# Ordering each strand's loads behind its own last product, and loading the RWKV bonus at the end of a pair's norm

## The chip, the cores and the metric

The kernel runs on one NeuronCore of one Trainium2 chip. The metric is the device time of one execution in microseconds (us). The kernel before takes 959.26 us, the median of 3 runs between 958.56 and 960.78 us. Its engines are TensorE (PE, with the load of its stationary operand shown apart as PEld), VectorE (DVE), ScalarE (ACT), GpSimd (POOL) and SyncE (SP), which here does little but issue transfers.

## What is computed

A hybrid decoder block on one sequence of 512 tokens and a width of 1024, in fp32. One input projection feeds two head groups: eight heads of sparse attention (compressed, selected and window branches with gates) and eight heads of RWKV-7 time mixing. Their outputs go through one output projection `w_out`; then come cross-attention into 256 memory tokens, a SwiGLU feed-forward part and a final norm.

```
h   = rms_norm(x, g1)
nsa = attention(q, k_cmp, v_cmp, k_sel, v_sel, k_win, v_win, gates)   # 8 heads
rw  = rwkv7(h)                 # state chain over time, group norm, + bonus, * gate
x   = x + concat(nsa, rw) @ w_out
x   = x + cross_attention(rms_norm(x, gx), rms_norm(mem, gm) @ w_kv_x) @ w_o_x
x   = x + swiglu(rms_norm(x, gf));  out = rms_norm(x, g_final)
```

The bonus of RWKV is a term of each head pair that is computed early, stored to DRAM (tile `bdr`), and added at the end of that pair's norm.

## The kernel before, in words

All of x stays on the chip. Weights come in blocks of 512 KB. A block has a raw tile `w` (two buffers), and is split into two halves: ScalarE casts it to `wh` (line 339) and VectorE subtracts to get `wl` (line 340); `wh` and `wl` have two buffers each. A product with a weight is three matmuls (line 207): high by high, high by low, low by high. A raw buffer is free for another load when the `wl` of its block is done, and a `wh` or `wl` buffer is free when TensorE has made the last product with it.

The order of work is written by a planner in the program (class `Threads`). The work is a set of generators, called strands: the bulk strand (all weight products in a fixed list), one for each attention unit, one for the RWKV inverse and chain, one for the memory tokens, and more. At each `yield` the planner takes the strand of highest priority that is ready, on a clock that it adds up from estimated product times. `pin` puts each TensorE instruction behind the one before it of the same strand (`mine[th.cur]`) and remembers it as the last of any strand (`last[0]`). These are edges of order only, for the list scheduler that writes the five instruction streams; they are no semaphores on the chip. `now` gives such an edge to a DMA. It is used by `wload` (every weight load, line 373), by the stores and loads of the bonus (lines 650 and 848), by the gate weight `gup` (line 844) and by a few smaller loads.

All these DMAs are issued by SP in one stream. Around 200 us the bulk strand ends the input projection (`pj`); the RWKV inverse stores its result to DRAM (`ydr`, `xdr`, lines 729 and 730) and loads it back in another layout (`AM`, `X`, lines 742 and 738). Small products `lt` and `y` follow, and then the chain of eight steps (`ch`, `zy`). From 300 us the bulk strand makes K of the memory tokens (`kx`, 8 blocks) and then V (`vx`, 4 blocks shown below), beside the attention units (`ps` scores, `pt` transposes, `pv` values; `S` the probabilities on ScalarE and VectorE) and the four RWKV norms (line 842 on). Then comes `w_out` (`acc`), whose first accumulators use the PSUM banks of `vx`. The x rows for the residual (`xr`, 4 times 512 KB, line 1317) are loaded by SP between the second and the third block of `w_out`.

Of the kernel before, what the change touches and what calls it, by code (L numbers as in the profile page):

```python
# [14 lines left out]
T = 512  # L15
# [112 lines left out]
def _body(ctx, tc, I, out, dbg=None, upto=99, mark=lambda s: None):  # L128
    nc = tc.nc
# [13 lines left out]
    def mk(tag, bufs, pool=None):  # L143
        def f(shape=(128, 512), dt=F32, n=tag):
            return (pool or pp).tile(list(shape), dt, tag=tag, bufs=bufs, name=nm(n))
        return f
# [9 lines left out]
    tU = mk("U", NU)  # L156
# [9 lines left out]
    th = Threads(mark, lambda n: tc.high_priority(n) if n else nullcontext(), Q=NQ - 7, T=NT, U=NU, K=KU, S=2, A=2)  # L166
# [4 lines left out]
    def after(ins, first):  # L171
        tc.add_manual_dep(ins.ins, first.ins.name,
                          mybir.DependencyInfo(mybir.DependencyClass.NoSync, mybir.DependencyReason.DATA), reason="order")
        return ins

    last, mine = [None], {}
# [8 lines left out]

    def now(ins):

        return after(ins, last[0]) if last[0] is not None else ins

    def free(ap):  # L190
        n = 1
# [4 lines left out]
    def mm(o, l, r, start, stop):  # L196
        m, n = free(l), free(r)
        if l.dtype == F32R:
            c = (0.055 if m <= 64 else 0.107) if n <= 128 else n * 0.000422
        elif m <= 32:  # L200
            c = 0.04
        elif m <= 64:
            c = max(0.08, n * 0.0009 + 0.02)
        else:
            c = max(0.214, n * 0.00168)
        th.cols.append((th.clock, n * l.shape[0] / 128 * (1 if l.dtype == F32R else F4)))
        return pin(PE.matmul(o, lhsT=l, rhs=r, start=start, stop=stop, skip_group_check=True), c)  # L207
# [130 lines left out]
    def split(H, L, src, eng=None):  # L338
        seq(A, A.copy(H, src))  # L339
        i = (eng or V).tensor_sub(L, src, v32(H))  # L340
        if not eng:
            seq(V, i)
# [22 lines left out]
    def qpair(n):  # L365
        t = tQ([128, 2, 512], F32R, n=n)
        return t[:, 0, :], t[:, 1, :]

    def wload(parts, kt, cols, dst=None):

        w = tW([128, kt, cols], n="w")
        for sl, c0, s in parts:
            now(nc.sync.dma_start(w[sl, :, c0:c0 + s.shape[2]], s))

        def halves(eng=None):
            h, l = dst or (tH([128, kt, cols], F32R, n="wh"), tL([128, kt, cols], F32R, n="wl"))
            with th.ahead(PR.get("split", 0)):
                split(h, l, w, eng)
            return h, l
        return halves  # L380
# [170 lines left out]
    def bsum(x, n, al):  # L551

        H, L = al(dt=F32R, n="bh"), al(dt=F32R, n="bl")
        split(H, L, x)
        yield 2.5
        p = pS(n=n)
        mm(p, bones_r, H, True, False)
        mm(p, bones_r, L, False, True)
        yield p
# [11 lines left out]
    bdr = dp.tile([4, 128, 512], F32, name="bdr")  # L571

    def rwkv_pair(j):
# [74 lines left out]
        v_ = rkv[j, 2]  # L648
        V.tensor_mul(t, p, v_)
        now(nc.sync.dma_start(bdr[j], t))  # L650
        th.free(T=1)
        yield dict(Q=2)

        am2 = []
        for e in range(2):
            am = tQ([128, 8, 128], n="AM")
            sl = slice(e * 64, e * 64 + 64)
            for hf in range(2):
                p = pB(n="sc")
                for c in range(4):  # L660
                    cc = hf * 4 + c
                    for o in range(2):
                        mm(p[o * 64:o * 64 + 64, c * 128:(c + 1) * 128], bk[sl, cc, o ^ e, :], ar[sl, cc, :], True, True)
                V.tensor_tensor(am[:, hf * 4:hf * 4 + 4, :], p.rearrange("p (c t) -> p c t", c=4),
                                mask2.rearrange("p (o t) -> p o t", o=1).broadcast_to([128, 4, 128]), op=ALU.mult)
                yield 0
            am2.append(am)
            for hh in range(2):
                now(nc.sync.dma_start(ndv[hh, e, j], am[e * 64 + hh * 32:e * 64 + hh * 32 + 32, :, hh * 32:hh * 32 + 32]))
# [109 lines left out]
    def chain():  # L779
        yield "vt"  # L780

        def own(q):

            for c in (2 * q, 2 * q + 1):
                for j, e, o in HEADS:
                    r = slice(64 - o, 128 - o)
                    mm(pE[o:o + 64, c % 2, j, :], AM[j][e][r, c, 0:64], VT[c // 4][r, c % 4, j, :], True, True)
            z = tU([128, 2, 4, 64], n="zv")
            A.copy(z, pE)
            return z  # L790

        yield "vg"
        yield dict(A=1)
        pE = pA([128, 2, 4, 64], n="zy")
        zv = own(0)
        yield CH_LAG
        p = pC([128, 2, 4, 64], n="ch")
        S = None
        for c in range(8):

            uv = tU([128, 2, 4, 64], n="uv")
            G.tensor_copy(uv[64:128, 0], VT[c // 4][64:128, c % 4])
            G.tensor_copy(uv[0:64, 1], VT[c // 4][0:64, c % 4])
            if c > 0:
                for j, e, o in HEADS:
                    mm(p[o:o + 64, 0, j, :], AR[j][o:o + 64, c, 0:64], S[o:o + 64, j, :], True, True)
                Z = t1([128, 4, 64], n="Z")
                V.tensor_add(Z, p[:, 0], zv[:, c % 2])
            else:
                Z = zv[:, 0]  # L810
            if c % 2 == 1 and c < 7:
                zv = own(c // 2 + 1)
            if c > 0:
                yield CH_LAG
            for j, e, o in HEADS:
                mm(p[o:o + 64, 1, j, :], AM[j][e][o:o + 64, c, 0:64], Z[o:o + 64, j, :], True, True)
            V.tensor_copy(uv[0:64, 0], p[0:64, 1])
            A.copy(uv[64:128, 1], p[64:128, 1])
            if c > 0:
                for j, e, o in HEADS:  # L820
                    mm(pE[o:o + 64, c % 2, j, :], S[o:o + 64, j, :], AR[j][o:o + 64, c, 64:128], j == 0, False)
            yield CH_LAG

            Sn = None
            if c < 7:
                for j, e, o in HEADS:
                    mm(p[o:o + 64, 0, j, :], BKt[j][:, c, e, :], uv[:, e, j, :], True, True)
                Sn = t1([128, 4, 64], n="S")
                if c == 0:
                    V.tensor_copy(Sn, p[:, 0])  # L830
                else:
                    G.tensor_tensor(Sn, S, WC[:, :, c:c + 1].broadcast_to([128, 4, 64]), op=ALU.mult)
                    V.tensor_add(Sn, p[:, 0], Sn)
            for j, e, o in HEADS:
                mm(pE[o:o + 64, c % 2, j, :], uv[:, e, j, :], AM[j][e][:, c, 64:128], c == 0, True)
            A.copy(VT[c // 4][:, c % 4], pE[:, c % 2])
            S = Sn
            yield CH_LAG
        th.done("chain", 1.0)
        th.free(Q=16, U=4, A=1)  # L840

        yield dict(Q=1)
        gup = tQ([128, 512], n="gup")
        now(nc.sync.dma_start(gup, I["rwkv_g_up"][0]))
        for j in range(4):
            yield dict(U=3, T=2)
            bon, sq, rs = tU(n="bon"), tU(n="ysq"), tU(n="rs")
            now(nc.sync.dma_start(bon, bdr[j]))
            h2 = [slice(0, 256), slice(256, 512)]
            c4 = lambda x: x.rearrange("p (c t) -> p c t", c=4)  # L850
            for h in range(2):
                A.activation(c4(sq[:, h2[h]]), VT[h][:, :, j, :], AF.Square)
            bs = bsum(sq, "var", tT)
            yield next(bs) + 1.0
            yield dict(s=1)
            p = next(bs)
            th.free(T=2)
            A.activation(rs, p, AF.Ln, bias=kst[:, 1:2], scale=1.0 / 64)
            A.activation(rs, rs, AF.Exp, scale=-0.5)
            for h in range(2):  # L860
                V.tensor_mul(c4(rs[:, h2[h]]), c4(rs[:, h2[h]]), VT[h][:, :, j, :])
            V.tensor_scalar(rs, rs, col("rwkv_lnx_w", j), col("rwkv_lnx_b", j), op0=ALU.mult, op1=ALU.add)
            G.tensor_tensor(rs, rs, bon, op=ALU.add)
            yield 6.0
            yield dict(s=1)
            p = pS(n="g")
            mm(p, gup[:, j * 128:(j + 1) * 128], sgd, True, True)
            V.tensor_mul(rs, p, rs)
            yield dict(Q=1)
            oT[4 + j] = qpair("oT")  # L870
            split(*oT[4 + j], rs)
            th.free(U=3)
            th.done(f"o{4 + j}", 4.0)
        th.free(Q=3)
# [765 lines left out]
```

## Time and profile before

| | us |
|---|---|
| median of the runs | 959.26 |
| the profiled execution's own time | 957.83 |
| its span, first to last instruction | 955.5 |
| TensorE busy | 910.5 (95%) |
| VectorE busy | 508.4 (53%) |
| ScalarE busy | 401.2 (42%) |
| GpSimd busy | 81.7 (9%) |

The span is 2.33 us shorter than the time of the same execution; these lie before the first and behind the last instruction. A row of a timeline is one instruction, or several alike in a row (x2), with its start, its duration, the engine, the source line and the tiles (out<-in); the bracket at its end is the idle time of the engine before it and what ended it. A row of a window gives for each engine how long it was busy in that stretch. TensorE's clock is shown as a share of full speed.

### The profile page before, as it was taken

What the parts mean: (1) busy time and instruction counts of PE and PEld (TensorE: products, weight loads), DVE (VectorE), ACT (ScalarE), POOL (GpSimd) and SP (SyncE); (2) the same over time, 40 slices, a digit from 0 to 9 for tenths busy, and PEclk for the clock granted to TensorE, in tenths of its full rate; (3) what the DMA queues carried; (4) which work ended last, traced back from release to release, by engine and by line L of the source; (5) the groups of instructions that cost most, each with busy time, mean ns of one, the idle gap of its engine ahead of it and who ended that gap; (6) DMA issues with size and microseconds to landing.
All of it is one profiled execution on the core that took longest, in us unless ns stands there. A gap on an engine that the chain in (4) does not pass through costs nothing.

```text
span 955.5 us, 14534 instructions
## 1 busy us (share of the span) xinstructions
PE 910.5 (95%) x5797; PEld 741.0 (78%) x5797; DVE 508.4 (53%) x991; ACT 401.2 (42%) x738; POOL 81.7 (9%) x128
## 2 busy tenths in 40 slices
PE   6999999999999988799899999999999999999997
PEld 4778777777778766666788888888888888888885
DVE  5366676788566776356655555444343343422235
ACT  4455444347567886234444433332333323212121
POOL 5121110000240010001200002000000000000002
PEclk9999999999999999999999999999999999999999
DMA  7222445636203111754431141333333333242332
GB/s 229 60 63 70 128 108 144 174 89 133 91 2 101 35 56 45 220 176 153 134 88 46 65 139 39 110 89 91 109 88 110 89 90 109 88 131 89 95 105 88
DMA packets 125405, 97.19 MB, mean 102 GB/s; under 512 B 23531, under 2 KB 109873, under 8 KB 125339
## 3 DMA queue, kind: packets, MB, share of 16 engines
q1 hardware_dynamic: 122714, 91.80, 33.2%
q10 hardware_dynamic: 2624, 4.48, 1.7%
q8 instruction: 45, 0.74, 0.3%
q14 instruction: 22, 0.17, 0.1%
HBM read 90.22 MB, written 4.48 MB: 99 GB/s over the span
## 4 chain that ended last, share of the span: by engine, by line
PE 76%; DVE 7%; ACT 6%; DMA 5%; issue 3%; POOL 2%; SPq 0%; POOLq 0%; ACTq 0%; DVEq 0%
PE pj L207 41%; PE acc L207 14%; DMA w<-in_w_out_dram 3%; PE pv L207 2%; DVE wl L340 2%; ACT wh L339 2%; PE sc L207 2%; PE pt L211 2%; PE ps L207 1%; PE vg L207 1%; PE ch L207 1%; DMA w<-in_w_kv_x_dram 1%; PE kx L207 1%; PE xs L207 1%; PE xo L207 1%
## 5 line engine op out<-in xcount | busy, mean ns | idle before, releaser
L207 PE MATMUL pj<-xn,wh 128*128 128x512 f32 (+1 forms) x1280 | 294.3, 378 | 0.5 <-DVE xn L340 0.5
L340 DVE TENSOR_TENSOR wl<-w,wh 128x1024 fp32r<-128x1024 f32 (+1 forms) x130 | 158.4, 1219 | 203.7 <-ACT wh L339 118.9
L207 PEld LDWEIGHTS pj<-xn,wh 128*128 128x128 f32 x1280 | 227.9, 190 | 46.0 <-issue 2.9
L339 ACT CAST wh<-w 128x1024 fp32r<-128x1024 f32 (+1 forms) x131 | 136.9, 1045 | 284.7 <-PE pj L207 144.6
L207 PE MATMUL pj<-xn,wl 128*128 128x512 f32 (+1 forms) x640 | 155.3, 379 | 0.0
L207 PEld LDWEIGHTS pj<-xn,wl 128*128 128x128 f32 x640 | 114.2, 189 | 22.0 <-issue 1.6
L207 PE MATMUL acc<-wh,hid 128*128 128x512 f32 x288 | 68.2, 389 | 0.0
L207 PEld LDWEIGHTS acc<-wh,hid 128*128 128x128 f32 x288 | 54.1, 188 | 11.2
L1475 DVE SCALAR_TENSOR_TENSOR th<-th,pj 128x512 f32<-128x512 f32 x22 | 15.1, 688 | 75.7 <-PE pj L207 75.7
L207 PE MATMUL acc<-wh,oT 128*128 128x512 f32 x128 | 34.6, 410 | 7.1 <-ACT wh L339 4.5
L1105 ACT ACTIVATE S<-S,mx 128x128 f32<-128x128 f32 (+3 forms) x64 | 35.3, 553 | 4.3 <-DVE mx L1103 4.2
L207 PEld LDWEIGHTS acc<-wh,oT 128*128 128x128 f32 x128 | 23.5, 192 | 15.8 <-ACT wh L339 7.9
L207 PE MATMUL acc<-wl,hid 128*128 128x512 f32 x144 | 35.6, 389 | 0.0
L1536 POOL TENSOR_TENSOR xr<-xr,gain 128x512 f32<-128x512 f32 x4 | 5.2, 1290 | 345.4 <-DVE ss L1533 345.4
L1103 DVE CUSTOM_DVE_ANT_0 S<-ps,Bt 128x128 f32<-128x128 f32 (+3 forms) x64 | 29.7, 484 | 8.5 <-PE ps L207 8.3
L207 PE MATMUL ps<-K,q 128*128 128x512 f32 (+2 forms) x96 | 30.1, 395 | 3.4 <-DVE mx L1103 2.3
L207 PEld LDWEIGHTS acc<-wl,hid 128*128 128x128 f32 x144 | 27.0, 188 | 5.6
L207 PE MATMUL pv<-S,Vt 128*64 128x128 f32 x320 | 30.6, 284 | 0.3 <-ACT S L1146 0.2
L211 PE MATMUL pt<-ident,S 128*128 128x128 f32 x160 | 25.8, 280 | 4.2 <-ACT S L1146 4.2
L339 ACT CAST hid<-th 128x512 fp32r<-128x512 f32 x22 | 13.7, 621 | 31.7 <-DVE th L1475 31.7
L280 POOL TENSOR_TENSOR ss<-ss,kst 128x1 f32<-128x1 f32 x14 | 7.7, 552 | 208.3 <-DVE ss L279 208.3
L211 PEld LDWEIGHTS pt<-ident,S 128*128 128x128 f32 x160 | 18.1, 140 | 9.4 <-ACT S L1146 5.3
(298 smaller groups left out, 1303.2 us busy)
## 6 DMA issues: line engine op xcount, KB each, us to landing
w<-in_w_gate_dram SPq DMA_DIRECT2D x22, 512.0 KB, 3.9
w<-in_w_up_dram SPq DMA_DIRECT2D x22, 512.0 KB
w<-in_w_down_dram SPq DMA_DIRECT2D x22, 512.0 KB, 3.4
w<-in_w_in_dram SPq DMA_DIRECT2D x18, 512.0 KB, 5.4
w<-in_w_kv_x_dram SPq DMA_DIRECT2D x16, 512.0 KB, 4.6
w<-in_w_out_dram SPq DMA_DIRECT2D x16, 256.0 KB, 3.9
w<-in_w_out_dram SPq DMA_DIRECT2D x8, 512.0 KB, 5.0
w<-in_w_q_x_dram SPq DMA_DIRECT2D x8, 512.0 KB, 3.9
```

Source lines behind the costliest of these rows:

```text
L207: return pin(PE.matmul(o, lhsT=l, rhs=r, start=start, stop=stop, skip_group_check=True), c)
L211: return pin(PE.transpose(o, i, idn), 0.109 if i.shape[0] > 64 else 0.056)
L280: G.tensor_tensor(ss[:, 1:2], ss[:, 0:1], mhalf, op=ALU.pow)
L339: seq(A, A.copy(H, src))
L340: i = (eng or V).tensor_sub(L, src, v32(H))
L1103: V.tensor_tensor_reduce(out=s, in0=p[:, br - b0], in1=Bt[:, a, n - 1::-1], scale=-1.0, scalar=3e38, op0=ALU.add, op1=ALU.min, accum_out=m ...
L1105: A.activation(s, s, AF.Exp, bias=mx[:, a, br + 1:br + 2], scale=-1.0, accum_out=sm[:, a, br + 1:br + 2])
L1475: V.scalar_tensor_tensor(t, t, 0.5, p, op0=ALU.mult, op1=ALU.mult)
L1536: G.tensor_tensor(x, x, gf[0][:, cs], op=ALU.mult)
```

## The change

`now` orders a DMA behind the last product of the strand that issues it (`mine[th.cur]`), and behind the last product of any strand only where its own has none. In the norm of an RWKV pair the buffer and the load of the bonus are asked for just before the bonus is added, so that the norm begins with two buffers of that pool instead of three.

```diff
     def now(ins):
 
-        return after(ins, last[0]) if last[0] is not None else ins
+        own = mine.get(th.cur, last[0])
+        return after(ins, own) if own is not None else ins
...
         for j in range(4):
-            yield dict(U=3, T=2)
-            bon, sq, rs = tU(n="bon"), tU(n="ysq"), tU(n="rs")
-            now(nc.sync.dma_start(bon, bdr[j]))
+            yield dict(U=2, T=2)
+            sq, rs = tU(n="ysq"), tU(n="rs")
...
             V.tensor_scalar(rs, rs, col("rwkv_lnx_w", j), col("rwkv_lnx_b", j), op0=ALU.mult, op1=ALU.add)
+            yield dict(U=1)
+            bon = tU(n="bon")
+            now(nc.sync.dma_start(bon, bdr[j]))
             G.tensor_tensor(rs, rs, bon, op=ALU.add)
```

No instruction is added or taken away; the streams change their order. In the rows below the first number in a name counts the program's tiles and is the same in both kernels where the place is the same; lines of the changed kernel stand one to three lower.

SP, from the last loads of the input projection on, in the kernel before (`in_w_in` is the input projection, `in_w_kv_x` the weight of kx and vx):

```order
L373 DMA w_321_1835<-in_w_in_dram 128x8x64 x2
L373 DMA w_325_1882<-in_w_in_dram 128x8x64 x2
L729 DMA ydr_1840<-yb_288_1526 128x1024
L730 DMA xdr_1842<-nb_287_1525 64x1024
L742 DMA AM_132_671<-ydr_1840 32x8x32 x2
L738 DMA X11_360_2034<-xdr_1842 32x16x32
L742 DMA AM_178_915<-ydr_1840 32x8x32 x2
L738 DMA X11_360_2034<-xdr_1842 32x16x32
```

And in the changed kernel:

```order
L374 DMA w_321_1835<-in_w_in_dram 128x8x64 x2
L374 DMA w_325_1882<-in_w_in_dram 128x8x64 x2
L374 DMA w_377_2119<-in_w_kv_x_dram 128x8x128
L730 DMA ydr_1840<-yb_288_1526 128x1024
L731 DMA xdr_1842<-nb_287_1525 64x1024
L743 DMA AM_132_671<-ydr_1840 32x8x32 x2
L739 DMA X11_360_2034<-xdr_1842 32x16x32
L743 DMA AM_178_915<-ydr_1840 32x8x32 x2
```

The first kx weight, w_377, now stands ahead of the store ydr; before, it stood behind the last load AM, fourteen rows on. Further down, the third kx weight moved ahead of the memory's gain, and each of the four bonus loads (before: two ahead of a kx weight and two together) now stands behind one kx weight, in turn.

ScalarE at the same place in the kernel before (S_342 and S_344 are exponentials of one attention unit, wh_407 is the cast of w_377):

```order
L1105 ACTIVATE S_342_1955,sm_338_1940<-S_342_1955,mx_337_1939 128x256
L1105 ACTIVATE S_344_1965,sm_338_1940<-S_344_1965,mx_337_1939 128x256 x2
L1090 ACTIVATE pc_347_1985,sm_346_1984<-pc_347_1985,mx_345_1983 128x23 x2
L1146 COPY S_334_1910<-pt_354_2009 128x256
L1105 ACTIVATE S_350_2001,sm_346_1984<-S_350_2001,mx_345_1983 128x384
```

And in the changed kernel:

```order
L1108 ACTIVATE S_342_1955,sm_338_1940<-S_342_1955,mx_337_1939 128x256
L340 CAST wh_407_2396<-w_377_2119 128x1024
L1108 ACTIVATE S_344_1965,sm_338_1940<-S_344_1965,mx_337_1939 128x256 x2
L1093 ACTIVATE pc_347_1985,sm_346_1984<-pc_347_1985,mx_345_1983 128x23 x2
L1108 ACTIVATE S_350_2001,sm_346_1984<-S_350_2001,mx_345_1983 128x384
L1149 COPY S_334_1910<-pt_354_2009 128x256
```

The cast wh_407 now stands between the two pairs of exponentials; before, it stood behind the copies of AM that open the chain.

VectorE at the end of the attention, in the kernel before (wl_693 is of the last kx block, wl_698 and wl_701 are of the first two vx blocks, S_672 and S_674 are copies for the last attention unit):

```order
L1148 COPY S_672_3965<-pt_689_4068 128x512
L340 TENSOR_TENSOR wl_693_4112<-w_681_4017,wh_692_4111 128x1024
L1148 COPY S_674_3973<-pt_691_4105 128x512
L340 TENSOR_TENSOR oT_696_4146<-pv_638_3825,oT_696_4146 128x512
L340 TENSOR_TENSOR wl_698_4154<-w_694_4115,wh_697_4153 128x1024
L340 TENSOR_TENSOR kx_511_3148<-kx_695_4117,kx_511_3148 128x2x256
L340 TENSOR_TENSOR wl_701_4186<-w_699_4157,wh_700_4185 128x1024
```

And in the changed kernel:

```order
L341 TENSOR_TENSOR wl_693_4112<-w_681_4017,wh_692_4111 128x1024
L1151 COPY S_672_3967<-pt_689_4060 128x512
L341 TENSOR_TENSOR wl_698_4154<-w_694_4115,wh_697_4153 128x1024
L1151 COPY S_674_3975<-pt_691_4105 128x512
L341 TENSOR_TENSOR oT_696_4146<-pv_636_3825,oT_696_4146 128x512
L341 TENSOR_TENSOR wl_701_4186<-w_699_4157,wh_700_4185 128x1024
L341 TENSOR_TENSOR kx_511_3148<-kx_695_4117,kx_511_3148 128x2x256
L341 TENSOR_TENSOR wl_706_4206<-w_702_4189,wh_705_4205 128x1024
```

The subtraction wl_698 moved ahead of the last copy S_674 and of oT_696, and wl_701 ahead of the split of kx; on ScalarE the casts wh_697 and wh_700 moved with them.

## Rows read from the trace of the kernel before

**Rows 1.** Page of the profile, its first lines (busy us, share of the span).

```profile
span 955.5 us, 14534 instructions
...
PE 910.5 (95%) x5797; PEld 741.0 (78%) x5797; DVE 508.4 (53%) x991; ACT 401.2 (42%) x738; POOL 81.7 (9%) x128
```

**Rows 2.** Windows: stretch, length, each engine busy, granted clock, DMA share, GB/s.

```profile
240.00:260.00 20.00, 19.94 (x453) 15.72 (x453) 11.11 (x28) 11.32 (x28) 5.40 (x11) 1.00 0.30 102
300.00:380.00 80.00, 73.54 (x576) 58.90 (x575) 54.38 (x173) 65.33 (x155) 6.76 (x9) 1.00 0.17 50
380.00:400.00 20.00, 16.30 (x67) 12.61 (x66) 9.19 (x10) 6.96 (x9) 0.00 (x0) 0.93 0.69 219
395.00:400.00 5.00, 4.43 (x13) 3.34 (x14) 2.34 (x3) 1.05 (x1) 0.00 (x0) 0.72 1.04 407
```

**Rows 3.** Waits of PE, 300 to 440 us (total, times, longest).

```profile
PE acc L207 <- ACT wh L339: 4.5, 6, 2.3
...
PE vx L207 <- DVE kx L340: 1.0, 1, 1.0
```

**Rows 4.** Timeline of SP, 195 to 260 us (start, duration, then the instruction).

```profile
199.69 0.99 SPq L373 DMA_DIRECT2D w<-in_w_in_dram  x2
215.71 0.34 SPq L729 DMA_DIRECT2D ydr<-yb  x1
...
232.78 2.00 SPq L373 DMA_DIRECT2D w<-in_w_kv_x_dram  x2
```

**Rows 5.** Timeline of VectorE, 202 to 217 us.

```profile
202.18 1.22 DVE L340 TENSOR_TENSOR wl<-w,wh 128x1024 fp32r<-128x1024 f32 x1
...
216.03 1.10 DVE L726 COPY nb<-yb 64x1024 f32<-64x1024 f32 x1
```

**Rows 6.** Timeline of ScalarE, 214 to 250 us.

```profile
214.62 0.51 ACT L1105 ACTIVATE S<-S,mx 128x256 f32<-128x256 f32 x1 [0.85 <-DVE mx L1103]
...
246.82 1.04 ACT L339 CAST wh<-w 128x1024 fp32r<-128x1024 f32 x1
```

**Rows 7.** Timeline of TensorE, 214 to 230 us.

```profile
215.51 1.67 PE L207 MATMUL pj<-xn,wl 128*128 128x512 f32 x5
...
227.39 0.55 PE L211 MATMUL pt<-ident,S 128*128 128x128 f32 x3 [1.32 <-ACT S L1146]
```

**Rows 8.** Waits of SP over the whole span.

```profile
SPq L848 <- DVE oT L340: 22.7, 2, 17.6
```

**Rows 9.** GpSimd's bonus add, all four by line (min/median/max ns, first and last start).

```profile
L863 POOL TENSOR_TENSOR rs<-rs,bon x4: 1288/1288/2051, 313.4 to 367.7; 128x512 f32<-128x512 f32 x4
```

**Rows 10.** Timeline of ScalarE, 376 to 406 us.

```profile
392.61 1.04 ACT L339 CAST wh<-w 128x1024 fp32r<-128x1024 f32 x1 [3.47 <-DMA w<-in_w_out_dram]
...
404.28 2.05 ACT L339 CAST wh<-w 128x1024 fp32r<-128x1024 f32 x2 [7.02 <-DMA w<-in_w_out_dram]
```

**Rows 11.** Timeline of VectorE, 355 to 406 us.

```profile
376.31 0.69 DVE L1148 COPY S<-pt 128x512 f32<-128x512 f32 x1 [1.74 <-PE pt L211]
...
380.30 1.22 DVE L340 TENSOR_TENSOR wl<-w,wh 128x1024 fp32r<-128x1024 f32 x1 [0.26 <-ACT wh L339]
```

**Rows 12.** Timeline of SP, 383 to 402 us.

```profile
388.00 3.53 SPq L373 DMA_DIRECT2D w<-in_w_out_dram  x4
391.58 3.00 SPq L1317 DMA_DIRECT2D xr<-in_x_dram  x4
394.94 3.94 SPq L373 DMA_DIRECT2D w<-in_w_out_dram  x3
```

**Rows 13.** Timeline of TensorE, 355 to 408 us.

```profile
395.57 2.73 PE L207 MATMUL acc<-wh,oT 128*128 128x512 f32 x8 [2.67 <-DVE vx L340]
398.09 1.91 PE L207 MATMUL acc<-wl,oT 128*128 128x512 f32 x4
...
402.01 1.07 PE L207 MATMUL acc<-wl,oT 128*128 128x512 f32 x4
405.38 2.11 PE L207 MATMUL acc<-wh,oT 128*128 128x512 f32 x8 [2.30 <-ACT wh L339]
```

## The prediction

> **What bounds the kernel now.** I read the page first: TensorE is busy 910.5 of 955.5 us [rows 1], so a change pays only where TensorE waits. The change moves loads, casts and subtractions that lie between 200 and 440 us, so I then read the windows of that stretch. They are unlike one another. From 240 to 260 us, where the RWKV chain starts, TensorE is busy 19.94 of 20 us: nothing can be won there, only lost. From 300 to 380 us it is busy 73.54 of 80, so 6.46 us lie open, and ScalarE beside it is busy 65.33 of 80: what TensorE waits for there comes out of ScalarE's queue. From 380 to 400 us it is busy 16.30 of 20, and in the last five of these at a granted clock of 0.72, between the two levels of 1.2 and 2.4 GHz, while the transfers run at 407 GB/s [rows 2]. The list of TensorE's waits, the third view, says what ends the late ones: the w_out products wait 4.5 us in six pieces for casts of weights [rows 3], and the casts in turn wait for transfers [rows 10]. Before 300 us TensorE works on products and small chains at once; behind 440 us nothing is moved.
>
> A word on the basis. The terms below are taken from one execution of 957.83 us, whose span is 955.5. The median of the runs, 959.26, is 1.43 higher; I add the sum to the median, since the result is a median too. About 0.2%, or 1.9 us, is what a measurement of this kernel can tell from no change.
>
> **Part one, the first kx weight.** In the kernel before, its load stands on SP behind the whole reload of the inverse and is issued at 232.78 us. Its buffer is free at 202.18 + 1.22 = 203.40, when the subtraction of the block that had it is done [rows 4, 5]. In the changed order it stands right behind the last input weight (issued at 199.69) and ahead of the store at 215.71 [rows 4], so it leaves some 29 us earlier, and it is over before the store, so the store pays nothing. What costs is the cast that follows it. It now stands in ScalarE's queue between two pairs of exponentials, of which the second began at 214.62 [rows 6]. The cast needs a buffer that TensorE still reads: the high products of the projection end where the low ones begin, at 215.51 [rows 7]. So the cast runs from 215.51 to about 216.55 (1.04 each [rows 6]), and the exponentials behind it are 216.55 - 214.62 = 1.9 us late, with all that waits for them on VectorE: the copy for the store xdr, at 216.03 before [rows 5], among it. How much reaches TensorE is not in the trace: nothing, if it has projection products to make meanwhile; all 1.9, if it stands still. It did stand still there once, for 1.32 us behind a copy of S [rows 7], so the cover is thin. I take 0.7, nearer to zero, as the low products of the projection lie just behind 215.51.
>
> **Part two, the start of the chain.** The cast of 1.04 at 246.82 [rows 6] and its subtraction (1.22, as [rows 5]) leave this place, but the next block's cast takes it, one copy earlier, and the work on the memory tokens comes forward between the chain's steps. TensorE idles 0.06 us there [rows 2], which is all that can be won. What can be lost is about one cast and one subtraction in front of copies that the chain waits for, 1.04 + 1.22 = 2.3. I take 0.5, near the full window.
>
> **Part three, 300 to 380 us.** Both kernels make the same products here, and up to the first kx product TensorE's order comes to the same amounts of each. Behind it the kx blocks, the four norms and the last attention units are mixed anew. Two casts of kx weights come a good deal earlier and stand together ahead of the exponentials of the last but one unit, 2 x 1.04 = 2.1 us on ScalarE; against that, a block more is ready to fill the gaps. No row prices a new mixture. The bounds are half of the open 6.46 us to either side, -3.2 and +3.2, and I take 0, since the number of fillers and of ScalarE's instructions is the same.
>
> **Part four, into w_out.** The subtraction for the first vx block ran at 380.30, behind a copy at 376.31 and the split of the last attention output [rows 11]. It now stands ahead of both, so that it can be done by about 376.3, and the load that waits for its buffer leaves up to 381.5 - 376.3 = 5.2 us earlier. The next subtraction now stands ahead of the split of kx, for which TensorE waits 1.0 us [rows 3]: that wait can grow by up to 1.22, and I take 0.5. Each later load hangs on a product of TensorE as well, so that of the 5.2 us about one subtraction, 1.2 to 1.3, arrives at the w_out loads at 388.00 and at the x rows behind them at 391.58 [rows 12]. The first w_out product, which waits 2.67 us [rows 13], then starts about 0.8 earlier, 1.3 from the load less 0.5 from the split. The third block is the test. Its load was issued at 394.94, behind four x rows of 512 KB [rows 12], and its cast ran at 404.28, 9.3 us later; the first w_out load, issued at 388.00, was cast at 392.61, 4.6 later [rows 10, 12]. So what is won before it is kept only as far as the x rows leave earlier. Term: -0.8; bounds -2.7 (the whole first wait) and +0.5.
>
> The first two blocks ran in the stretch at 0.72: eight products in 2.73 against 2.11 later, four in 1.91 against 1.07 [rows 2, 13], so 0.62 + 0.84 = 1.46 us went to the clock. I do not count them as won, since the third block waits for its load either way. The Trainium skill ("TensorE: Matmul & The Clock Gate", section "HAM oscillation — how this bites in real kernels") says that a wait for a transfer can drop the clock, and that the work behind it then starts cold. The drop behind the 2.67 us wait agrees. By that rule a shorter wait would give back the 1.46 too, and the sum below would be -1.1 instead of +0.4; that is the first rival.
>
> **Part five, the bonus.** SP stood 22.7 us in all at two of its old loads [rows 8], in order behind them. The four adds run from 313.4 to 367.7 [rows 9], 18 us apart on average. In the new order a bonus load needs the buffer that the add before it frees, so SP can issue it some 18 us ahead of its own add, and a load of that size lands in about a quarter of that (4.6 us for the w_out load of 256 KB above, an estimate). It costs nothing as long as no kx weight needs SP meanwhile; the weights that now stand behind a bonus wait for a subtraction of their own anyway. If the cover were gone, an add would be late by those 4.6, at the end of the norm, off TensorE's path until w_out asks for the fourth to seventh block.
>
> The Trainium skill ("DMA: Bandwidth & Descriptors", section "Rules for kernel authors") advises to issue a transfer early and to wait late. The bonus does the opposite in the program's text, and by that rule alone the four adds would come 4 x 4.6 = 18.4 us later in all. The 18 us between the adds speak against it: the place in the text is not the time of issue.
>
> **The sum.** +0.7 + 0.5 + 0 - 0.8 + 0 = +0.4: 958.2 on the profiled basis, 959.7 as a median. With all bounds at one end it would be -6.0 or +7.9, which do not fall together.
>
> **The rivals.** *The lead of the weights is kept (faster).* The whole first wait of w_out goes (-2.67), and with it the slow stretch (-1.46), if the x rows leave early enough to let the third block's load land before TensorE asks. With +0.7, +0.5 and the +0.5 of the split it is -2.4: 956.8. For it: the first vx load has 5.2 us of lead. Against it: the later loads hang on TensorE's own products, and 2 MB of x rows still stand in front of the third block.
>
> *Casts in front of exponentials (slower).* ScalarE works in order, so each weight that lands early puts its cast ahead of exponentials that TensorE waits for: 1.9 at 214 us in full, and 2.1 for the two casts ahead of the last but one unit, where ScalarE is at 65.33 of 80. With +0.5 and -0.8 it is +3.7: 963.0. It decides from the moment TensorE has no kx product left while a unit's exponentials stand behind a cast. Against it: in the kernel before, 73.54 of 80 us were filled in spite of such casts.
>
> *The loads move on SP alone (no change).* If the buffers held the loads as much as the order did, the new order delays and advances casts that had slack: 0, 959.3. Against it: the first weight does gain 29 us.
>
> **How the numbers follow.** My forecast has 0.32, the fast rival 0.29, the slow one 0.26, and the third 0.13. Forecast and third rival lie within 0.2% of 959.26 (957.3 to 961.2), mostly; so do a few cases of the others, and as many of the forecast's leave it on the fast side: faster 0.32, same 0.42, slower 0.26. The likeliest one's own range is 957.9 to 961.5. The range for 8 in 10 takes in both signed rivals and a good part of part three's bounds: 955.0 to 963.0.
>
> **What would show it.** In the changed profile: a kx weight issued near 203.4; its cast near 215.5 and exponentials behind it near 216.5; the window from 240 to 260 still above 19 us of TensorE; from 300 to 380 about 73.5; the second vx load near 376.5 instead of 381.5; w_out's first wait near 1.5 instead of 2.67, and a third-block wait at least as long as 2.30. The forecast is wrong if the window from 300 to 380 differs by over 2 us, if the third block no longer waits, or if TensorE stands still for over a microsecond around 216 to 222.

## The result, and the profile after

The changed kernel takes 969.25 us, the median of 4 runs between 968.20 and 972.94 us; the kernel before took 959.66 us beside it (4 runs, 958.56 to 960.78). The ratio is 1.0095, with a 95% interval of 1.007 to 1.012: slower by 9 to 10 us (9.6 between the medians). That is outside the forecast range, and 6 us above what the slow rival gave.

The profiled execution took 972.94 us. The first lines of its page answer to [rows 1]:

```profile
span 970.6 us, 14531 instructions
...
PE 922.2 (95%) x5797; PEld 750.8 (77%) x5797; DVE 508.5 (52%) x991; ACT 401.0 (41%) x738; POOL 78.7 (8%) x128
```

TensorE is busy for 11.7 us more with the same 5797 matmuls, and the span is 15.1 us longer. So products ran slower, not only later. To find where, I laid the last lt product, the first kx product and the last product of the kernel side by side. Of the 15.1 us, 5.2 arise before 85 us: 0.9 near 20 to 30 us, and 4.3 near 70 to 80 us, where this one execution ran ten microseconds at half clock. One window there, first of the kernel before, then of the changed one (stretch, length, busy time of PE, PEld, DVE, ACT and POOL, granted clock, share of DMA, GB/s):

```profile
75.00:80.00 5.00, 5.00 (x29) 4.13 (x29) 4.53 (x6) 1.67 (x3) 1.13 (x2) 1.00 0.41 105
75.00:80.00 5.00, 5.00 (x43) 4.53 (x36) 4.29 (x5) 0.00 (x0) 0.00 (x0) 0.50 0.47 112
```

The runs e3 and e7 below, whose TensorE order is there that of the kernel before, show such a stretch at that place too, and so do e2 and e5, whose medians are no slower than before; so I leave it out. Another 0.3 us arise up to the last lt product, 9.3 from there to the first kx product, and 0.3 behind it. So the loss sits in one stretch, the start of the chain. The window of that stretch in the kernel before:

```profile
242.20:289.80 47.60, 46.61 (x915) 37.48 (x908) 32.12 (x99) 32.03 (x83) 16.21 (x31) 1.00 0.16 49
```

The same in the changed kernel, and three more of its windows, which the text below uses:

```profile
247.70:304.60 56.90, 53.30 (x916) 41.61 (x908) 32.47 (x98) 31.12 (x83) 15.04 (x31) 0.85 0.11 37
315.00:395.00 80.00, 71.67 (x571) 58.71 (x566) 54.36 (x172) 65.02 (x153) 5.89 (x9) 1.00 0.19 57
250.00:255.00 5.00, 2.13 (x46) 1.68 (x44) 0.53 (x2) 0.76 (x3) 0.00 (x0) 0.67 0.30 120
255.00:260.00 5.00, 5.00 (x21) 3.27 (x20) 0.32 (x1) 1.66 (x3) 0.00 (x0) 0.50 0.02 3
```

The stretch is 56.90 us long instead of 47.60. TensorE's idle time in it rose from 47.60 - 46.61 = 0.99 to 56.90 - 53.30 = 3.60 us, and its busy time, with the same products, by 53.30 - 46.61 = 6.69 us. The clock says why: in the window from 255 to 260 us it is 0.50, the lower of its two levels (1.2 GHz), and 0.67, a mean of both, in the one ahead of it; in the kernel before, the whole stretch is at 1.00. Stall 2.6, slow clock 6.7: together the 9.3.

What stalled? The y products at the head of the chain, in the changed kernel, on TensorE (start, duration, instruction, idle time before it and its end):

```profile
250.53 0.43 PE L208 MATMUL y<-AM,LT 32*32 32x32 f32 x14
253.83 0.64 PE L208 MATMUL y<-AM,LT 32*32 32x32 f32 x16 [2.87 <-issue]
...
258.02 2.05 PE L208 MATMUL pj<-xn,wl 128*128 128x512 f32 x4
```

and in the kernel before:

```profile
244.81 0.85 PE L207 MATMUL y<-AM,LT 32*32 32x32 f32 x30
...
248.27 0.73 PE L207 MATMUL pj<-xn,wl 128*128 128x512 f32 x2
```

In the kernel before, thirty y products run in one piece. In the changed one, TensorE stands still for 2.87 us in the middle of them, put down to "issue": none of the semaphores that the profile shows was late. Behind it four projection products take 2.05 us instead of two in 0.73, that is 0.51 each instead of 0.37, the mark of the lower clock. The waits of TensorE in the whole stretch of the changed kernel (total, times, longest) are two:

```profile
PE y L208 <- issue: 2.9, 1, 2.9
PE tr L212 <- DVE pcT L1137: 0.7, 1, 0.7
```

The second, 0.7 us, is in the kernel before as well. So no wait for a late cast or copy is left there to explain the 9.3 us.

What was missing is the instructions themselves. The traces list transfers of instructions, 16 KB each, on a queue of their own (q8): 45 of them, one for about 260 of TensorE's 5797 products and as many weight loads, while the page lists at most 991 instructions for any other engine; so it is TensorE's stream that they bring. In the kernel before, the transfer for the place in question lies in the 1.5 us from 242.3, with no other traffic beside it:

```profile
DMA packets 1, 0.02 MB, mean 11 GB/s; under 512 B 0, under 2 KB 0, under 8 KB 0
...
q8 instruction: 1, 0.02, 4.8%
```

In the changed kernel, TensorE comes to the same instruction of its stream at 248.31 us. The transfers of the three microseconds around that time, 247.7 to 250.7, are 0.98 MB of data on q1 and no instruction packet:

```profile
DMA packets 271, 0.98 MB, mean 328 GB/s; under 512 B 31, under 2 KB 31, under 8 KB 271
...
q1 hardware_dynamic: 271, 0.98, 95.7%
```

In the three microseconds behind them, from 250.7, the instruction packet is there:

```profile
q1 hardware_dynamic: 84, 0.27, 23.1%
q8 instruction: 1, 0.02, 2.1%
```

From the packet records, the instruction transfer starts at 242.82 in the kernel before, when TensorE is at that instruction, and at 251.43 in the changed one, 3.12 us after TensorE has passed it. The data that ran instead are the memory tokens. The timeline of SP in the changed kernel:

```profile
208.66 0.37 SPq L374 DMA_DIRECT2D w<-in_w_kv_x_dram  x1
...
237.85 2.27 SPq L374 DMA_DIRECT2D w<-in_w_kv_x_dram  x2
245.32 0.35 SPq L1202 DMA_DIRECT2D mem<-in_norm_mem_g_dram  x1
245.72 0.90 SPq L1205 DMA_DIRECT2D mem<-in_mem_dram  x2
```

and in the kernel before:

```profile
238.54 0.35 SPq L1199 DMA_DIRECT2D mem<-in_norm_mem_g_dram  x1
250.87 0.37 SPq L373 DMA_DIRECT2D w<-in_w_kv_x_dram  x1
251.29 1.05 SPq L1202 DMA_DIRECT2D mem<-in_mem_dram  x2
```

with this wait of SP between the first two of these rows:

```profile
SPq L373 <- DVE wl L340: 11.9, 1, 11.9
```

In the kernel before, SP issued the gain at 238.54, and then waited 11.9 us with the third kx weight until a subtraction had freed its buffer, at 250.87, so that the memory rows behind it on SP went out at 251.29, when the y products were over. In the changed kernel the first weight is loaded at 208.66 and subtracted early, so the third weight no longer waits; the gain and both rows, 1.5 MB, go out from 245.32 to 246.62, as soon as the projection products that read their buffer are done, and run while TensorE goes through the lt and y products and needs its next instructions. The wait that the change took away had kept the memory rows off TensorE's instructions.

### The profile page after: what moved, and what is told of

Read it like the earlier page. It is cut to its first block, busy times and chain, and to the rows that moved or that the text cites. A ratio compares the mean times of both kernels' runs of the same rounds, so it can differ in the third digit from the quotient of the medians.

```text
span 970.6 us, 14531 instructions
## 1 busy us (share of the span) xinstructions
PE 922.2 (95%) x5797; PEld 750.8 (77%) x5797; DVE 508.5 (52%) x991; ACT 401.0 (41%) x738; POOL 78.7 (8%) x128
## 4 chain that ended last, share of the span: by engine, by line
PE 49%; DMA 3%; DVE 3%; POOL 1%; issue 1%; ACT 1%; SPq 0%; POOLq 0%; ACTq 0%; DVEq 0%
PE pj L208 29%; PE acc L208 16%; DMA w<-in_w_out_dram 2%; PE xs L208 1%; PE xo L208 1%; DVE wl L341 1%; ACT wh L340 1%; PE vx L208 1%; PE tr L212 1%; DMA w<-in_w_up_dram 1%; POOL xr L1539 1%; DMA gain<-in_norm_x_g_dram 0%; DMA w<-in_w_kv_x_dram 0%; POOL xs L295 0%; PE xpt L212 0%
## 5 line engine op out<-in xcount | busy, mean ns | idle before, releaser
L1478 DVE SCALAR_TENSOR_TENSOR th<-th,pj 128x512 f32<-128x512 f32 x22 | 15.1, 688 | 75.7 <-PE pj L208 75.7
L208 PEld LDWEIGHTS pv<-S,Vt 128*64 128x64 f32 x320 | 20.2, 139 | 6.9 <-issue 2.3
```

Source lines behind the costliest of these rows:

```text
L1478: V.scalar_tensor_tensor(t, t, 0.5, p, op0=ALU.mult, op1=ALU.mult)
```

## The experiments

The theory: TensorE's next block of instructions is fetched late, because the gain and the memory rows are in flight; the stall brings the clock down. Rivals: the bonus load costs the time (A); the casts ahead of exponentials, and the new order at the chain's start, cost it (B).

**e1, the change of `now` alone.** The bonus is loaded as before.

```diff
-        return after(ins, last[0]) if last[0] is not None else ins
+        own = mine.get(th.cur, last[0])
+        return after(ins, own) if own is not None else ins
```

> The change of `now` alone, the bonus loaded as before. Theory (TensorE's block of instructions is fetched late, since the gain and the two memory rows, 1.5 MB, are in flight at the start of the chain): this kernel has the same order of SP up to the memory loads, so it is slow by the same 9 to 10 us, about 969, with an idle stretch of TensorE of nearly 3 us put down to issue among the y products. Rival A (the bonus load at the end of the norm costs the time): 959 to 960. Rival B (casts ahead of exponentials starve the chain): about 969 too.

967.59 us beside 958.86, ratio 1.0098 (1.0062 to 1.0134). The wait of TensorE at the y products (total, times, longest):

```profile
PE y L208 <- issue: 2.9, 1, 2.9
```

The change of `now` alone gives a loss of the same size, and the same stall.

**e2, the bonus alone.**

```diff
-            yield dict(U=3, T=2)
-            bon, sq, rs = tU(n="bon"), tU(n="ysq"), tU(n="rs")
-            now(nc.sync.dma_start(bon, bdr[j]))
+            yield dict(U=2, T=2)
+            sq, rs = tU(n="ysq"), tU(n="rs")
...
+            yield dict(U=1)
+            bon = tU(n="bon")
+            now(nc.sync.dma_start(bon, bdr[j]))
             G.tensor_tensor(rs, rs, bon, op=ALU.add)
```

> The move of the bonus alone, `now` as before. Theory and rival B: 958.5 to 960.5, no idle stretch among the y products. Rival A: 965 or more.

960.41 us beside 958.86, ratio 1.0010 (0.9991 to 1.0029), so rival A falls. There is a small wait at the same place:

```profile
PE y L207 <- issue: 0.2, 1, 0.2
```

Here the instruction transfer started 0.27 us late. From 243.7 to 245.0 us it is the only packet:

```profile
DMA packets 1, 0.02 MB, mean 13 GB/s; under 512 B 0, under 2 KB 0, under 8 KB 0
...
q8 instruction: 1, 0.02, 4.2%
```

So no data traffic delayed this one by its 0.27 us; what did stays open. The interval leaves room for a cost of up to 2.8 us, which part five had put at nothing.

**e3, the kernel before with the memory rows early.** TensorE, VectorE, ScalarE and GpSimd have the streams of the kernel before, instruction for instruction; only SP issues the memory rows ahead of the third kx weight, which is issued behind them.

```diff
+        th.done("memld")                       # in mem_load, behind the row loads
...
-        return ld, run
+        return (ld, run, "memld") if k == 2 else (ld, run)     # in kx_item
```

> The kernel before, with the third kx weight held until the memory rows are issued, so that the gain and both rows go out together near 239 us and are in flight when the y products of the chain's start run (242 to 246 us). No cast is moved ahead of an exponential. Theory: the fetch of TensorE's next block of instructions comes late, TensorE stands still for 1 to 4 us among the y products, and the clock falls behind it: 963 to 970. If the rows are over before the fetch is asked for: no change. Rival B: 959 to 960.

966.30 us beside 958.86, ratio 1.0087 (1.0057 to 1.0117). SP issued the loads at

```profile
242.24 0.35 SPq L1199 DMA_DIRECT2D mem<-in_norm_mem_g_dram  x1
242.63 0.90 SPq L1202 DMA_DIRECT2D mem<-in_mem_dram  x2
257.85 0.38 SPq L373 DMA_DIRECT2D w<-in_w_kv_x_dram  x1
```

and TensorE did this:

```profile
248.51 0.47 PE L207 MATMUL y<-AM,LT 32*32 32x32 f32 x17
250.42 0.38 PE L207 MATMUL y<-AM,LT 32*32 32x32 f32 x13 [1.44 <-issue]
...
254.62 1.22 PE L207 MATMUL pj<-xn,wl 128*128 128x512 f32 x2
```

Two loads, some 12 us earlier (this execution was 3.7 us late by then), with no engine's order changed but SP's, cost 7.4 us, most of what the whole change costs: a stall of 1.44 us, and half clock behind it (0.61 us for a projection product). This is the run that tells most, since rival B has nothing to offer for it. The transfer of instructions started 1.37 us late.

**e4, the changed kernel with gain and rows held.** GpSimd writes one column of the tile behind its first copies of the chain, and the loads wait for that.

```diff
-            G.tensor_copy(uv[0:64, 1], VT[c // 4][0:64, c % 4])                # in chain()
+            uvc[0] = G.tensor_copy(uv[0:64, 1], VT[c // 4][0:64, c % 4])
...
     def mem_load(dep):
+        yield "c0"                             # th.done("c0") in chain(), behind step 0
         tmp = tX([128, 3, 1024], n="mem")
         gm = tmp[:, 2]
+        dep = last[0]
+        after(G.memset(tmp[:, :, 0:1], 0.0), uvc[0])    # behind that copy
```

> The changed kernel, with the gain and the memory rows held by a small write of GpSimd that stands behind its first copies of the chain (about 4 us later than now). All else, the casts ahead of exponentials too, as in the changed kernel. Theory: the stall among the y products and the slow clock behind it go, 958.5 to 961.5. Rival B: 967 to 970. If the rows then hold the fetch of the following block instead: 962 to 967.

962.46 us beside 958.86, ratio 1.0056 (1.0036 to 1.0076). The loads were held longer than I meant, by some 20 us:

```profile
266.23 0.35 SPq L1209 DMA_DIRECT2D mem<-in_norm_mem_g_dram  x1
266.63 0.90 SPq L1212 DMA_DIRECT2D mem<-in_mem_dram  x2
```

The stretch from the last lt to the first kx product:

```profile
242.50:293.90 51.40, 47.16 (x911) 37.56 (x901) 31.60 (x98) 30.43 (x83) 15.90 (x32) 1.00 0.15 46
```

Two of TensorE's waits in it, of five, none of them put down to issue:

```profile
PE ch L208 <- ACT uv L819: 1.1, 2, 0.6
PE pt L212 <- ACT S L1151: 1.0, 1, 1.0
```

The stall is gone and the clock is 1.00: some 6 of the 9 to 10 us come back by the medians, nearer 4 by the ratios. The median missed the theory's band by a microsecond; it lies in the one that I gave to a later fetch being held, but no wait for issue bears that out. Idle time in the stretch is 51.40 - 47.16 = 4.24 us, 3.25 more than before, in small waits for ScalarE and VectorE at the chain's start. So rival B may hold a part, some 3 us, unless the late memory rows cost it; e4 doesn't tell these apart. In the changed kernel itself these waits are not there: they show only once the stall is gone.

**e5, the first kx weight by the old rule.** The rest of the change stays; the memory rows are ordered behind the last weight load, as they stood.

```diff
+            lwd[0] = ld = nc.sync.dma_start(w[sl, :, c0:c0 + s.shape[2]], s)
+            after(ld, last[0]) if old else now(ld)      # old: kx block 0
...
+            after(after(<row load>, dep), lwd[0])       # in mem_load
```

> The changed kernel with the first kx weight alone ordered by the old rule, and the memory rows ordered behind the third kx weight as in the kernel before; the later weights and the bonus as changed. The third weight waits for the first one's subtraction near 250 us, so the memory rows go out behind the y products. Theory: no late fetch and no cast ahead of the exponentials at 214 us; what is left of the change is its later part: 957.5 to 960. If the later part costs the 3.6 us that were left when the memory rows were held: 961.5 to 963.5.

959.98 us beside 959.75, ratio 1.0008 (0.9988 to 1.0028). The same stretch:

```profile
244.00:293.10 49.10, 46.21 (x904) 36.74 (x897) 33.38 (x99) 32.35 (x84) 15.30 (x31) 1.00 0.15 49
```

Idle time 49.10 - 46.21 = 2.89 us, still 1.9 above before, at full clock; behind the first kx product the profiled execution won back 1.4. This run puts back two things at once, the place of the first weight and that of the memory rows, and with both back no loss is measured (the interval ends at 2.7 us). What e4 had left may come from the first weight's own place or from the late rows; e5 doesn't tell these apart either.

**e6, only the two rows held.** As e4, with the gain left as in the changed kernel.

> The changed kernel with only the two memory rows (1 MB) held by the small write of GpSimd; the gain (0.5 MB) goes out when its buffer is free, as in the changed kernel. Theory (the later the fetch, the longer the stall): a third of the bytes delays the fetch by about 1 us instead of 3.1, TensorE comes to the end of its block no earlier than the fetch lands, no stall or one under 0.5 us, no slow clock: 961 to 963.5, as with all three held. If any of these loads at that time is enough: 965 or more.

963.21 us beside 959.75, ratio 1.0046 (1.0022 to 1.0069). SP issued the gain and, much later, the rows:

```profile
245.46 0.35 SPq L1206 DMA_DIRECT2D mem<-in_norm_mem_g_dram  x1
271.32 0.82 SPq L1212 DMA_DIRECT2D mem<-in_mem_dram  x2
```

The stretch from the last lt to the first kx product:

```profile
247.90:298.50 50.60, 47.44 (x912) 37.70 (x902) 31.52 (x98) 30.55 (x83) 14.95 (x32) 1.00 0.12 38
```

The instruction transfer started on time (0.04 us late, at 248.48), there was no stall, and the clock stayed at 1.00. But the gain was all but over by then. These are the data packets from 245.4 to 248.47, and those from 248.47 to 250:

```profile
q1 hardware_dynamic: 135, 0.51, 53.8%
...
q1 hardware_dynamic: 9, 0.02, 2.8%
```

So e6 shows that the gain alone, issued 3 us ahead, is out of the way in time. It doesn't show that 0.5 MB still in flight would do no harm.

**e7, the new rule from the end of the chain on.** TensorE's stream is that of the kernel before up to the kx products; on ScalarE one square of the first norm comes earlier, near 280 us.

```diff
-        own = mine.get(th.cur, last[0])
+        own = mine.get(th.cur, last[0]) if "chain" in th.ev else last[0]
```

> The new rule of `now` only once the chain is done, the old one before; the bonus as changed. All streams are those of the kernel before up to the first kx products. In the profiles so far the stretch from the first kx product to the end was 0.8 to 1.7 us shorter than before where memory was held. Theory (the late part of the change is a small gain, the chain's start is the loss): from the first lt product to the first kx product as before, and 0.8 to 1.7 less behind it: 957.5 to 959.5, against before in the same call. If the bonus costs what its single run showed behind the chain (1.9): 960 to 962.

958.57 us beside 958.57, ratio 0.9986 (0.9967 to 1.0005). The stretch is as before, 0.99 us of idle time:

```profile
247.40:294.80 47.40, 46.41 (x915) 37.37 (x908) 32.06 (x99) 32.30 (x84) 16.16 (x31) 1.00 0.16 50
```

The expected band held, but not the reason for it: from the first kx product to the last product this one execution was 0.4 us longer than before, where 0.8 to 1.7 less was expected. By the interval the late part of the change is worth between 3.2 us of gain and 0.5 of loss; neither this version nor e5 is shown to beat the kernel before.

## Why the prediction was wrong

**The step that failed is part two, the start of the chain.** It said: "What can be lost is about one cast and one subtraction in front of copies that the chain waits for, 1.04 + 1.22 = 2.3. I take 0.5". Measured, up to the first kx product, it is 9.3. The section on the change says that the third kx weight moved ahead of the memory's gain; I priced the casts that came forward, and not the loads behind them on SP, which the lines of [rows 4] leave out. The third weight had been the gate of the memory rows until 250.87; with the first weight subtracted early it held nothing. And I bounded a loss by the durations of the instructions that moved. A stall that halves the clock has no such bound: 2.6 us of idle time cost 6.7 us more at 0.50. Of the signs that the prediction named, the window from 240 to 260 failed: the one that answers to it, 245.5 to 265.5, has TensorE busy for 17.08 us, not above 19, at a clock of 0.66. None of the three signs of being wrong lies in this stretch.

How the pieces hang together is shown by four executions. The instruction transfer started late by 3.12 us (after), 3.05 (e1), 1.37 (e3) and 0.27 (e2), and the waits at the y products were 2.9, 2.9, 1.4 and 0.2 us; of these four, the first three had data in flight beside the transfer. In e4 to e7 it started within about 0.1 us of its place, and there was no such wait. TensorE took up its work 2.4 to 2.5 us after the start of the transfer each time, and in the kernel before it reached the same instruction 2.46 us after it: that kernel had next to no margin, which no row of its waits showed. The clock follows the stall: of the nine profiled executions, the three with a stall of over a microsecond are the only ones at half clock anywhere between 235 and 390 us.

**Part one was right in its mechanism; its size is not settled.** The first weight was loaded at 208.66; less the 5.2 us by which this execution was late by then, that is 203.46, forecast 203.40. Its cast stood in front of the exponentials:

```profile
219.78 1.05 ACT L340 CAST wh<-w 128x1024 fp32r<-128x1024 f32 x1 [0.57 <-PE pj L208]
220.73 0.51 ACT L1108 ACTIVATE S<-S,mx 128x256 f32<-128x256 f32 x1
```

They began at 220.73, less 5.2 is 215.5, 0.9 us late instead of 1.9. TensorE lost 0.3 up to the last lt product, forecast 0.7. But this low number owes something to luck, since the kernel before, in its profiled execution, lost time there to the clock:

```profile
210.00:215.00 5.00, 2.71 (x9) 2.00 (x8) 3.45 (x22) 4.15 (x18) 0.00 (x0) 0.79 0.01 2
```

By the clock records it ran 3.4 us at half clock from 212.9 us on. The changed kernel had no such stretch there, nor had e2 and e3, which have the old order and went from 210 us to the last lt product 1.3 and 1.4 us faster than the kernel before did. Beside those two the new order costs 1.6 to 1.7 us, most of the bound of 1.9. e7, of the old order too, had such a stretch again; so part one lies between 0.3 and 1.7.

**Part three was right.** From the first kx to the last kx product the changed kernel is 0.3 us longer (forecast 0). In the window from 315 to 395 above, which holds nearly the same work as that from 300 to 380 in [rows 2], TensorE was busy 71.67 us instead of 73.54; that is 1.9 less, just under the 2 us that I had set as a limit, and it did not show in the length of the stage.

**Part four was right step by step, up to the first w_out product.** TensorE in the changed kernel:

```profile
397.93 1.62 PE L208 MATMUL vx<-wh,mn 128*128 128x512 f32 x6 [1.66 <-DVE kx L341]
...
409.79 2.24 PE L208 MATMUL acc<-wh,oT 128*128 128x512 f32 x8 [1.18 <-DVE vx L341]
...
419.48 2.93 PE L208 MATMUL acc<-wh,oT 128*128 128x512 f32 x6 [3.83 <-ACT wh L340]
```

and SP beside it:

```profile
401.93 3.83 SPq L374 DMA_DIRECT2D w<-in_w_out_dram  x4
405.81 3.00 SPq L1320 DMA_DIRECT2D xr<-in_x_dram  x4
```

The wait for the split of kx grew from 1.0 [rows 3] to 1.66 (forecast: 0.5 more). The first w_out load left at 401.93, less the 15.1 us by which the changed kernel was late at its last kx product 386.8, 1.2 earlier than before, as forecast. The first wait of w_out fell from 2.67 [rows 13] to 1.18 (forecast near 1.5), the eight products behind it ran at full clock, and the third block waited 3.83 instead of 2.30, since its load stands behind the four x rows, issued from 405.81 on [rows 12]. From the last kx to the first w_out product the kernel won 0.9 us; the term was -0.8. The clock's 1.46 us, counted as not won, were not: the slow stretch came behind the third block's wait instead. But the 0.8 did not last, and the sum had it as kept: from the first w_out product to the last product of the kernel the changed one is 0.9 us longer. Half clock for another 3.4 us from 477 us on, by the clock records, is part of that. That the clock fell behind a wait here, and behind the stall of the y products, agrees with the Trainium skill ("TensorE: Matmul & The Clock Gate", section "HAM oscillation — how this bites in real kernels"), weighed in the prediction for w_out alone. What the page tells of are waits for a transfer of data; the stall here was for instructions. By that rule the loss of part two is more than its idle time; the window at 0.50 bears it out.

**Part five** had the bonus at nothing, and e2's interval holds that. Of the rivals, the slow one (+3.7) named ScalarE's queue. With the fetch out of the way e4 is 3.6 us above the kernel before by its median, 3.4 to 7.3 by its interval; how much of that is ScalarE's queue is open. The greater part of the loss, the late fetch and the clock behind it, is a mechanism that I had not listed.

## What to carry to other kernels

Before a load is set free, look at what waited behind it in the queue of its issuer: a wait can be the only thing that keeps a large transfer away from a burst of small products. Where TensorE runs many tiny products in a row, its own instructions are a stream that must be fed, and 1.5 MB in flight at that moment can starve it. Price a stall of TensorE together with the clock behind it, which here cost 3.8 to 6.7 us behind stalls of 1.4 to 2.9 us (TensorE's busy time in the stretch of e1, e3 and the changed kernel, less 46.61).

## What the runs showed of the hardware

TensorE's instructions come in transfers of 16 KB on a queue of their own, and 1.5 MB issued 2 to 3 us before one was due delayed it by 3.1 us, issued 3 to 4 us before by 1.4 us (e3). 0.5 MB issued 3 us before did not delay it, and had all but landed when it was due (e6). Such a wait shows in the profile as "issue", on no semaphore. The half clock behind the stall lasted 17.1 us in the changed kernel and 10.2 in e1 and e3, by the clock records, though e1's stall was as long as the first and e3's half of it; why one was longer is open. Stretches at half clock near 70 to 80 us, 6.8 to 10.2 us long by the same records, appeared in seven of the nine profiled executions, also in kernels that have TensorE's order of the kernel before up to there; each costs 2.8 to 4.4 us against the kernel before, which is why a single time of this kernel says little.
